# A double buffer of its own for the blocks of w_down in the up projection

## The chip, the cores and the metric

The kernel runs on one core of one Trainium2 chip. The metric is the time of one execution in microseconds of device time; three executions of the kernel before are at hand.

## The reference

One layer of a hybrid encoder block over 1024 tokens of width 1024: a convolution and attention mixer, a cross-attention into 256 memory tokens, and a gated MLP with 2816 hidden channels. Only the MLP is touched:

```python
def conv_gated_ffn(h, w_up, ffn_dw, ffn_dw_b, w_down):
    u = jnp.einsum("bsd,df->bsf", h, w_up)
    u = dwconv_centred(u, ffn_dw, ffn_dw_b)
    gate, val = u[..., :D_FF], u[..., D_FF:]
    return jnp.einsum("bsf,fd->bsd", jax.nn.gelu(gate, approximate=True) * val, w_down)
```

## The kernel before

Both projections of the MLP are done as two-by-two block products by Strassen's scheme: seven products of half-sized blocks in place of eight, paid for with sums and differences of blocks. Every float32 operand is split in a high and a low part and a block product takes three matmuls, on lines 97, 98 and 100.

The **up projection** runs in 22 rounds, one for each 128 gate and 128 value channels (`fi`). A round has seven products (against b11, b21, t2, t1, b22, t3 and t4, which are the token side's blocks and their sums). Each product has 4 steps of 3 matmuls, so a round has 84 matmuls. In the order of the program a round does this:

- `up_first(fi)` loads the gate weights `wg`, splits them (ScalarE copies the high part on line 758, GpSimd makes the low part on line 759) and runs the products b11 and b21.
- `up_operands(fi)` loads the value weights `wv`, forms sums of weight blocks on GpSimd (lines 791 to 794) and splits them (ScalarE on line 758, VectorE on line 759; the block `a22` on GpSimd).
- `down_load(fi)` loads 512 KB of `w_down` into a staging tile `wd` (line 748).
- `up_finish(fi - 1)` runs the five other products of the round before, adds them up on VectorE (line 819), applies the depthwise convolution of width 3 (lines 808 to 811), gelu and the product of gate and value (line 842), and stores the result in `act_d` (line 843).
- `down_sums(fi)` turns the four blocks of `w_down` into the four sums that the down projection will need: four subtractions of 128x256 elements in place on VectorE (line 754). It then stores them in `T_d` in DRAM (line 755). The down projection, after the 22 rounds, loads `T_d` again (line 892).

Four kinds of buffers matter. `raw` is a pool of three tiles of 512 KB, shared in the up projection by `wg`, `wv` and `wd`. `A` is a pool of 15 tiles of 1 MB: in the up projection 14 of them hold the split token operands (`b11h`, `b11l` and so on), and `acts`, the operand tiles of the down projection, and then `gF` come from the same pool, in the order of the program. `W` has seven tiles for split weights and for `u`. PSUM has four banks for the products (`psB`).

The order of the work is not that of the program alone. The program is planned ahead of time (`schedule_with_timeline_sim=True`): at each point of the planner's own estimate of time, an engine or the DMA queue of SyncE is given, of the instructions that are ready by that estimate, the one that stands earliest in the program. The order that comes out of it is fixed for each engine. On the chip each engine works its list off in order and waits at an instruction whose inputs or buffer are late. All DMAs here are issued from the one queue of SyncE (SP), in its order.

Of the kernel before, what the change touches and what calls it, by code (L numbers as in the profile page):

```python
# [8 lines left out]
F32 = mybir.dt.float32  # L9
# [8 lines left out]
NF = 22  # L18
# [15 lines left out]
def encoder_block(ctx: ExitStack, tc: tile.TileContext, x, xT, mem, w_a, w_q, w_kv, w_mkv, w_mqT,  # L34
                  w_mo, w_out, w_up, w_down, cols, rows, g10, rope, out):
    nc = tc.nc
# [10 lines left out]
    def A(shape, name, dt=F32R):  # L47
        return ap.tile([128] + shape, dt, tag="a", name=name)

    def raw(name):  # L50
        return rawp.tile([128, 1024], F32, tag="raw", name=name)
# [7 lines left out]
    def psB(name):  # L59
        return psp.tile([128, 512], F32, tag="B", name=name, bufs=4)  # L60
# [259 lines left out]
    for c in range(8):  # L320
        w = wsplit(w_mqT[c], f"wmq{c}")
        go = tmp("go")
        for g in range(2):
            p = psB("pg")
# [416 lines left out]

    T_d = drp.tile([NF // 2, 128, 4, 512], F32, name="T_d")

    wds = {}

    def down_load(fi):
        wds[fi] = raw("wd").rearrange("p (b n) -> p b n", b=4)
        nc.sync.dma_start(out=wds[fi], in_=w_down[fi // 2, :, :, fi % 2 * 256:fi % 2 * 256 + 256])

    def down_sums(fi):  # L750
        wd = wds.pop(fi)
        b11, b12, b22, b21 = [wd[:, b, :] for b in range(4)]
        for dst, in0, in1 in ((b11, b12, b11), (b12, b22, b12), (b22, b22, b11), (b21, b22, b21)):
            nc.vector.tensor_tensor(out=dst, in0=in0, in1=in1, op=ALU.subtract)  # L754
        nc.sync.dma_start(out=T_d[fi // 2, :, :, fi % 2 * 256:fi % 2 * 256 + 256], in_=wd)

    def a_split(dst, src, eng):
        nc.scalar.copy(out=dst[:, 0, :], in_=src)  # L758
# [12 lines left out]
    def up_first(fi):  # L771

        rg = rgs.pop(fi) if fi in rgs else load_raw(w_up[fi, 0], "wg")
        a1 = W([2, 2, 512], "a1")
        a_split(a1[:, 0], rg[:, H0], nc.gpsimd)
        a_split(a1[:, 1], rg[:, H1], nc.gpsimd)
        u = wp.tile([128, 2, 1024], F32, tag="w", name="u")
        q = tmp("q")
        p1, p2 = psB("p1"), psB("p2")
        product(p1, a1[:, 0], "b11")  # L780
        nc.scalar.copy(out=q[:, H0], in_=p1)
        product(p2, a1[:, 1], "b21")
        nc.vector.tensor_tensor(out=u[:, 0, H0], in0=p2, in1=q[:, H0], op=ALU.add)
        firsts[fi] = (rg, u, q)

    def up_operands(fi):

        rg, u, q = firsts.pop(fi)
        rv = load_raw(w_up[fi, 1], "wv")
        s12, s34 = tmp("s12"), tmp("s34")  # L790
        nc.gpsimd.tensor_tensor(out=s12[:, H0], in0=rv[:, H0], in1=rv[:, H1], op=ALU.add)
        nc.gpsimd.tensor_tensor(out=s12[:, H1], in0=s12[:, H0], in1=rg[:, H0], op=ALU.subtract)
        nc.gpsimd.tensor_tensor(out=s34[:, H0], in0=rg[:, H0], in1=rv[:, H0], op=ALU.subtract)
        nc.gpsimd.tensor_tensor(out=s34[:, H1], in0=rg[:, H1], in1=s12[:, H1], op=ALU.subtract)
        a2, a3 = W([2, 2, 512], "a2"), W([2, 2, 512], "a3")
        a_split(a2[:, 0], s12[:, H1], nc.vector)
        a_split(a2[:, 1], s12[:, H0], nc.vector)
        a_split(a3[:, 0], s34[:, H1], nc.vector)
        a_split(a3[:, 1], s34[:, H0], nc.vector)
        if fi % 2 == 0:  # L800
            a22[0] = W([2, 2, 512], "a22")
        a_split(a22[0][:, fi % 2], rv[:, H1], nc.gpsimd)
        ups[fi] = (a2, a3, a22[0][:, fi % 2], u, q)
# [11 lines left out]
    def up_finish(fi):  # L815
        a2, a3, a22_, u, q = ups.pop(fi)

        def add(dst, ps, other, op=ALU.add, swap=False):
            nc.vector.tensor_tensor(out=dst, in0=other if swap else ps, in1=ps if swap else other, op=op)  # L819

        p6, p5 = psB("p6"), psB("p5")
        if fi == 0:
            product(p5, a2[:, 1], "t1")
        product(p6, a2[:, 0], "t2")
        add(q[:, H0], p6, q[:, H0])
        if fi:
            product(p5, a2[:, 1], "t1")
        add(q[:, H1], p5, q[:, H0])
        p3 = psB("p3")
        product(p3, a3[:, 0], "b22")  # L830
        add(u[:, 0, H1], p3, q[:, H1])
        p7 = psB("p7")
        product(p7, a3[:, 1], "t3")
        add(q[:, H0], p7, q[:, H0])
        add(u[:, 1, H1], p5, q[:, H0])
        cg = conv3(fi, 0, u)
        nc.scalar.activation(out=u[:, 0], in_=cg, func=AF.Gelu_apprx_tanh)
        p4 = psB("p4")
        product(p4, a22_, "t4")
        add(u[:, 1, H0], p4, q[:, H0], op=ALU.subtract, swap=True)  # L840
        cv = conv3(fi, 1, u)
        nc.vector.tensor_tensor(out=u[:, 1], in0=u[:, 0], in1=cv, op=ALU.mult)
        nc.sync.dma_start(out=act_d[fi], in_=u[:, 1])
# [11 lines left out]
    for fi in range(NF + 1):  # L855
        if fi < NF:
            if fi >= UP_PRE:
                up_first(fi)
            up_operands(fi)
            down_load(fi)  # L860
        if fi:
            up_finish(fi - 1)
        if fi < NF:
            down_sums(fi)

# [205 lines left out]
```

## Time and profile before

| what | us |
|---|---|
| median of three executions | 1469.17 |
| lowest and highest of the three | 1468.13, 1473.19 |
| the profiled execution, its own time | 1470.58 |
| span of its profile (first to last instruction) | 1468.5 |
| TensorE (PE) busy in that span | 1391.3 |
| VectorE (DVE) busy | 1083.4 |
| ScalarE (ACT) busy | 699.1 |
| GpSimd (POOL) busy | 522.3 |

The engines work side by side, so the busy times don't add up to the span. 2.1 us of the profiled execution lie outside its span. The up projection takes about the stretch from 770 to 1250 us of the span.

### The profile page before, as it was taken

The numbers are of one execution on the slowest core, as the hardware profiler recorded it, in microseconds if no ns is written. First come the engines' busy times: TensorE is split into PE (matmuls) and PEld (weight loads), VectorE is DVE, ScalarE is ACT, GpSimd is POOL, SyncE is SP. The second block draws the span as 40 slices with busy tenths as digits, with TensorE's granted clock in tenths as the row PEclk, the third lists the DMA queues.
The fourth block names the chain that finished last, engine by engine and source line by source line (L and its number), as shares of the span: only waits on it lengthen the run. The fifth ranks groups of instructions, "written<-read, shape, count | busy, mean of one in ns | idle before, by whom it ended". The sixth has DMA issues, their size and how long they took to land.

```text
span 1468.5 us, 18850 instructions
## 1 busy us (share of the span) xinstructions
PE 1391.3 (95%) x7020; PEld 1168.7 (80%) x7020; DVE 1083.4 (74%) x1464; ACT 699.1 (48%) x1192; POOL 522.3 (36%) x508
## 2 busy tenths in 40 slices
PE   7999999889999999999997899999998999999996
PEld 5889988678988888888885677777787777888885
DVE  7599898899999534335468777777777678986576
ACT  6325653678888524334344433343344333544452
POOL 6628877711111414002136533444455441000003
PEclk9999999999999999999998999999999999999999
DMA  6416760000000424113222443343343348622325
GB/s 209 136 50 207 254 240 13 20 1 1 1 2 29 165 94 142 46 43 130 86 86 75 155 143 129 125 135 129 131 129 113 130 143 308 251 90 90 108 86 208
DMA packets 74059, 170.08 MB, mean 116 GB/s; under 512 B 9712, under 2 KB 32496, under 8 KB 73968
## 3 DMA queue, kind: packets, MB, share of 16 engines
q1 hardware_dynamic: 73968, 168.88, 34.2%
q8 instruction: 55, 0.90, 0.3%
q14 instruction: 36, 0.29, 0.1%
HBM read 124.82 MB, written 44.04 MB: 115 GB/s over the span
## 4 chain that ended last, share of the span: by engine, by line
PE 48%; DVE 20%; DMA 12%; issue 8%; POOL 7%; ACT 4%; SPq 1%; DVEq 0%; POOLq 0%; ACTq 0%
DMA wd<-in_w_down_dram 5%; PE yd L91 4%; PE yd L92 4%; PE yd L90 4%; PE y L98 4%; PE y L100 4%; PE y L97 4%; DVE wd L754 3%; PE pPT L81 3%; DMA T_d<-wd 2%; PE sc L100 2%; PE sc L97 2%; PE sc L98 2%; DVE u L819 2%; PE sp L524 2%
## 5 line engine op out<-in xcount | busy, mean ns | idle before, releaser
L295 DVE SCALAR_TENSOR_TENSOR cacc<-conv,col,cacc 128x1009 f32<-128x1009 f32 (+14 forms) x120 | 145.8, 1274 | 4.7 <-ACT cacc L242 4.4
L85 POOL TENSOR_SCALAR rt<-ss 128x1 f32<-128x1 f32 (+1 forms) x43 | 14.9, 347 | 367.6 <-DVE ss L899 228.3
L91 PE MATMUL yd<-op 128*128 128x512 f32 x308 | 119.9, 390 | 0.5 <-DVE op L899 0.5
L92 PE MATMUL yd<-op 128*128 128x512 f32 x308 | 119.7, 389 | 0.0
L758 ACT CAST a<-s 128x512 fp32r<-128x512 f32 x88 | 51.5, 619 | 114.4 <-PE p L100 53.8
L754 DVE TENSOR_TENSOR wd<-wd 128x256 f32<-128x256 f32 x88 | 63.8, 725 | 55.0 <-DMA wd<-in_w_down_dram 40.8
L759 POOL TENSOR_TENSOR a<-wg,a 128x512 fp32r<-128x512 f32 x44 | 61.0, 1406 | 102.5 <-ACT a L758 102.1
L90 PE MATMUL yd<-op 128*128 128x512 f32 x308 | 97.1, 389 | 0.0
L909 ACT CAST op<-acts 128x512 fp32r<-128x512 f32 x77 | 47.9, 622 | 97.7 <-PE yd L92 86.6
L899 DVE TENSOR_TENSOR op<-acts,op 128x512 fp32r<-128x512 f32 x77 | 52.9, 687 | 45.5 <-ACT op L909 45.4
L545 DVE TENSOR_TENSOR PL<-pPT,PH 128x512 fp32r<-128x512 f32 x128 | 82.7, 680 | 5.0 <-ACT PH L544 4.6
L527 DVE TENSOR_REDUCE nm<-sp 128x1 f32<-128x1024 f32 x64 | 78.0, 1219 | 3.2 <-PE sp L525 2.2
L809 DVE SCALAR_TENSOR_TENSOR c<-u,col,c 128x1023 f32<-128x1023 f32 x44 | 56.5, 1284 | 28.9 <-ACT c L808 28.9
L530 ACT ACTIVATE P<-sp,nm 128x1024 f32<-128x1024 f32 x64 | 72.2, 1129 | 8.8 <-PE pPT L81 5.1
L544 ACT CAST PH<-pPT 128x512 fp32r<-128x512 f32 x128 | 69.2, 593 | 13.5 <-PE pPT L81 12.8
L81 PE MATMUL pPT<-ident,P 128*128 128x128 f32 x512 | 69.5, 276 | 2.4 <-DVE PL L545 1.0
L759 DVE TENSOR_TENSOR a<-s,a 128x512 fp32r<-128x512 f32 x88 | 59.4, 694 | 12.3 <-ACT a L758 12.3
L91 PEld LDWEIGHTS yd<-op 128*128 128x128 f32 x308 | 57.8, 188 | 13.2 <-DVE op L899 1.3
L81 PEld LDWEIGHTS pPT<-ident,P 128*128 128x128 f32 x512 | 59.7, 142 | 10.6 <-DVE PL L545 3.1
L90 PEld LDWEIGHTS yd<-op 128*128 128x128 f32 x308 | 57.8, 188 | 12.0
L92 PEld LDWEIGHTS yd<-op 128*128 128x128 f32 x308 | 57.8, 188 | 12.0
L808 ACT ACTIVATE c<-u,col 128x1024 f32<-128x1024 f32 x44 | 53.2, 1209 | 26.9 <-DVE u L819 25.9
(341 smaller groups left out, 4401.0 us busy)
## 6 DMA issues: line engine op xcount, KB each, us to landing
wg<-in_w_up_dram SPq DMA_DIRECT2D x22, 512.0 KB, 3.7
wv<-in_w_up_dram SPq DMA_DIRECT2D x22, 512.0 KB, 4.3
wd<-in_w_down_dram SPq DMA_DIRECT2D x22, 512.0 KB, 3.9
T_d<-wd SPq DMA_DIRECT2D x22, 512.0 KB, 3.2
act_d<-u SPq DMA_DIRECT2D x22, 512.0 KB, 5.1
acts<-act_d SPq DMA_DIRECT2D x22, 512.0 KB, 8.3
st<-T_d SPq DMA_DIRECT2D x20, 512.0 KB, 3.7
wmkv_r<-in_w_mkv_dram SPq DMA_DIRECT2D x16, 512.0 KB, 4.2
```

The source lines that it names most:

```text
L81: nc.tensor.transpose(out=out_, in_=in_, identity=ident)
L90: nc.tensor.matmul(out=ps, lhsT=sh, rhs=mh, start=first, stop=False)
L91: nc.tensor.matmul(out=ps, lhsT=sh, rhs=ml, start=False, stop=False)
L92: nc.tensor.matmul(out=ps, lhsT=sl, rhs=mh, start=False, stop=last)
L97: nc.tensor.matmul(out=p, lhsT=sh, rhs=mh, start=first, stop=False)
L98: nc.tensor.matmul(out=p, lhsT=sh, rhs=ml, start=False, stop=False)
L100: ins = nc.tensor.matmul(out=p, lhsT=sl, rhs=mh, start=False, stop=last)
L295: nc.vector.scalar_tensor_tensor(out=acc[:, t0:t1_], in0=a[:, t0 + o:t1_ + o], scalar=cc(C_DW + c * 31 + j), in1=acc[:, t0:t1_], op0=ALU.m ...
L527: nc.vector.reduce_max(out=nm, in_=sp, axis=AX.X, negate=True)
L545: nc.vector.tensor_tensor(out=PL[dst], in0=p3, in1=f(PH[dst]), op=ALU.subtract)
L754: nc.vector.tensor_tensor(out=dst, in0=in0, in1=in1, op=ALU.subtract)
L759: eng.tensor_tensor(out=dst[:, 1, :], in0=src, in1=f(dst[:, 0, :]), op=ALU.subtract)
```

## The change

The blocks of `w_down` no longer come through the pool `raw`. One tile of the pool `A` becomes a double buffer `wd_b`, with one half for even and one for odd `fi`. The store to `T_d` is split off from the sums into `down_store`. The load for round `fi + 1` now stands behind the sums of round `fi` in the program, and the store of round `fi - 1` stands in round `fi`, between `up_operands(fi)` and `up_finish(fi - 1)`. The number of loads, sums and stores, and their sizes, stay as they are.

```diff
-    wds = {}
+    wd_b = A([2, 4, 256], "wd", F32)
+
+    def down_slice(dr, fi):
+        return dr[fi // 2, :, :, fi % 2 * 256:fi % 2 * 256 + 256]
 
     def down_load(fi):
-        wds[fi] = raw("wd").rearrange("p (b n) -> p b n", b=4)
-        nc.sync.dma_start(out=wds[fi], in_=w_down[fi // 2, :, :, fi % 2 * 256:fi % 2 * 256 + 256])
+        nc.sync.dma_start(out=wd_b[:, fi % 2], in_=down_slice(w_down, fi))
 
     def down_sums(fi):
-        wd = wds.pop(fi)
-        b11, b12, b22, b21 = [wd[:, b, :] for b in range(4)]
+        b11, b12, b22, b21 = [wd_b[:, fi % 2, b, :] for b in range(4)]
         for dst, in0, in1 in ((b11, b12, b11), (b12, b22, b12), (b22, b22, b11), (b21, b22, b21)):
             nc.vector.tensor_tensor(out=dst, in0=in0, in1=in1, op=ALU.subtract)
-        nc.sync.dma_start(out=T_d[fi // 2, :, :, fi % 2 * 256:fi % 2 * 256 + 256], in_=wd)
+
+    def down_store(fi):
+        nc.sync.dma_start(out=down_slice(T_d, fi), in_=wd_b[:, fi % 2])
...
             up_operands(fi)
-            down_load(fi)
-        if fi:
+        if fi == 0:
+            down_load(0)
+        else:
+            down_store(fi - 1)
             up_finish(fi - 1)
         if fi < NF:
             down_sums(fi)
+        if fi + 1 < NF:
+            down_load(fi + 1)
```

## Rows read from the trace of the kernel before

**Rows 1.** The page's head: span, then busy us, share and instructions per engine

```profile
span 1468.5 us, 18850 instructions
PE 1391.3 (95%) x7020; PEld 1168.7 (80%) x7020; DVE 1083.4 (74%) x1464; ACT 699.1 (48%) x1192; POOL 522.3 (36%) x508
```

**Rows 2.** Matmuls on t4h: duration ns min/median/max, first and last start in us

```profile
L97 PE MATMUL p<-t4h,a x88: 389/389/389, 807.3 to 1246.1; 128*128 128x512 f32 x88
```

**Rows 3.** Timeline of PE, four instructions: start us, us, line, idle before and releaser

```profile
813.03 0.50 PE L97 MATMUL p<-b11h,a 128*128 128x512 f32 x1 [2.90 <-ACT a L758]
...
1005.85 0.47 PE L97 MATMUL p<-b21h,a 128*128 128x512 f32 x1 [3.00 <-DVE q L819]
...
1112.65 0.39 PE L97 MATMUL p<-t2h,a 128*128 128x512 f32 x1
...
1123.53 0.39 PE L97 MATMUL p<-t4h,a 128*128 128x512 f32 x1
```

**Rows 4.** PE's waits from 780 to 1271 us: total us, times, longest

```profile
PE p L97 <- DVE q L819: 19.7, 9, 3.0
PE p L97 <- ACT a L758: 7.2, 4, 2.9
```

**Rows 5.** One stretch of 5 us: PE busy, granted clock, DMA share, GB/s

```profile
920.00:925.00 5.00, 1.99 (x6) 0.78 0.09 30
```

**Rows 6.** Timeline of DVE, two stretches

```profile
1000.50 1.29 DVE L809 SCALAR_TENSOR_TENSOR c<-u,col,c 128x1023 f32<-128x1023 f32 x1 [1.28 <-ACT c L808]
1003.57 1.54 DVE L754 TENSOR_TENSOR wd<-wd 128x256 f32<-128x256 f32 x1 [1.78 <-DMA wd<-in_w_down_dram]
1005.03 0.68 DVE L819 TENSOR_TENSOR q<-p,q 128x512 f32<-128x512 f32 x1
...
1066.70 0.95 DVE L899 TENSOR_TENSOR acts<-acts 128x512 f32<-128x512 f32 x1 [0.74 <-DMA acts<-act_d]
```

**Rows 7.** Timeline of POOL, two instructions

```profile
999.73 1.30 POOL L759 TENSOR_TENSOR a<-wv,a 128x512 fp32r<-128x512 f32 x1
...
1003.57 1.25 POOL L791 TENSOR_TENSOR s<-wv 128x512 f32<-128x512 f32 x1
```

**Rows 8.** Timeline of SP's queue: when each DMA was issued

```profile
4.47 1.52 SPq L422 DMA_DIRECT2D rope_t<-in_rope_dram  x2
...
791.13 0.66 SPq L748 DMA_DIRECT2D wd<-in_w_down_dram  x1
800.37 0.34 SPq L617 DMA_DIRECT2D wv<-in_w_up_dram  x1
...
808.41 0.34 SPq L617 DMA_DIRECT2D wg<-in_w_up_dram  x1
...
829.38 0.33 SPq L874 DMA_DIRECT2D acts<-act_d  x1
...
999.80 0.57 SPq L748 DMA_DIRECT2D wd<-in_w_down_dram  x1
...
1247.26 0.33 SPq L878 DMA_DIRECT2D gF<-in_rows_dram  x1
```

**Rows 9.** All instructions on wd: the sums' ns, DVE's wait before them, landing

```profile
L754 DVE TENSOR_TENSOR wd<-wd x88: 406/424/1539, 798.8 to 1215.8; 128x256 f32<-128x256 f32 x88
...
  DMA wd<-in_w_down_dram: 40.8, 15
...
DMA to landing us min/median/max: 3.2/3.7/7.9
```

**Rows 10.** DMA issues: count, KB each, median us from issue to landing

```profile
wd<-in_w_down_dram SPq DMA_DIRECT2D x22, 512.0 KB, 3.9
T_d<-wd SPq DMA_DIRECT2D x22, 512.0 KB, 3.2
```

**Rows 11.** 820 to 1220 us: busy of PE, PEld, DVE, ACT, POOL, clock, DMA share, GB/s

```profile
820.00:1220.00 400.00, 374.86 (x1600) 304.16 (x1599) 301.23 (x387) 152.60 (x213) 179.84 (x136) 0.98 0.40 132
```

**Rows 12.** The same stretch, the sums of line 754 alone: DVE busy first

```profile
820.00:1220.00 400.00, 57.64 (x80) 0.98 0.40 132
```

## The prediction

> **What bounds the kernel now.** I read the page first: PE is busy 95% of the span [rows 1], so a change can only gain where PE stands still or runs slowly. The change touches the up projection alone, so next I measured that stage by PE's own pace. In full flow, four products lie between the two last rows of the PE timeline: 48 matmuls in 1123.53 - 1112.65 = 10.88 us, 0.2267 us each [rows 3]. A round of 84 matmuls would take 19.04 us at that pace. The t4 products of the first and last round start at 807.3 and end their fourth step's first matmul at 1246.1 [rows 2]: between them lie 21 rounds and three steps, 1773 matmuls, which should take 401.9 us and take 438.8. **36.9 us are lost in the stage**, and a round takes 20.80 us. That is all that a perfect cure of the stage could give.
>
> Then I asked what ends PE's waits. The largest entry is "q L819", VectorE's add that frees a PSUM bank: 19.7 us in 9 waits, the longest 3.0; then weights that ScalarE had not split yet, 7.2 us in 4 [rows 4]. The rest of the 36.9 are smaller waits and slow running: in the 5 us around one such stop the granted clock averages 0.78 [rows 5].
>
> One stop shows the mechanism. PE waits 3.00 us before 1005.85 for the add q [rows 3]. On VectorE that add stands behind the first subtraction on `wd`, which waited 1.78 us for its load and then took 1.54 us [rows 6]. The load was issued at 999.80, while GpSimd was at the low part of a value weight block (`a<-wv`, from 999.73), whose reading frees a `raw` tile [rows 7, 8]. So `wd` gets its buffer late, lands late, and VectorE, which works in order, holds up an add that was ready. Over the stage VectorE waits 40.8 us in 15 places for `wd` [rows 9].
>
> **The change, part by part.**
>
> *Bytes and instructions.* 22 loads, 88 subtractions, 22 stores before and after: 0 us of work added or removed.
>
> *`raw` has one user less.* Two tiles a round instead of three use the three buffers. The start shows what that is worth: the second `wv` was issued only at 800.37, the third `wg` at 808.41, because the first `wd` had taken a buffer at 791.13 [rows 8], and PE then waited 2.90 us for the split of that `wg` [rows 3]. With the buffer free, `wv` moves to about 791 and `wg` to about 800, 8 to 9 us earlier, more than that wait. This is part of the 36.9, not in addition.
>
> *`wd_b` takes the 15th `A` tile.* The first half of the first `acts` was loaded into it at 829.38 [rows 8]. Now that load comes after the last store to `T_d`; it is needed at the down projection, beyond 1246, so 0 us while the last store is done well before. The first `wd` load must wait for the tile, until the token operands are split and the 15th tile is free: the first sums now start at 798.8 [rows 9], and a load issued there lands 3.9 us later [rows 10]. Between 0 and 3.9 us, once; I take 0, because it is weighed again in the next term.
>
> *The loads asked for a round ahead, the stores a round behind.* What the program says about rounds binds little, since the planner issues whatever is ready. Two rows show it: the position tables of the attention stage were loaded at 4.47, as their small buffer was free, and the first `acts` half at 829.38, some twenty rounds ahead of its place [rows 8]; VectorE even did a sum on `acts` at 1066.70, in the middle of the up projection, and waited 0.74 us for it [rows 6]. What held `wd` to its round was the shared pool, whose tiles go out in program order (`gF`, which waits for no result, was loaded only at 1247.26, behind the `acts` [rows 8]). With a buffer of its own nothing holds it. **So I expect the blocks to run ahead:** load, four sums, store, next load into the same half, as fast as it goes, in VectorE's gaps. From the rows: load 3.9 [rows 10], four sums at 57.64 / 80 = 0.72 us each, 2.9 [rows 12], store 3.2 [rows 10], together 10.0 us for a half, two halves in turn, a block per 5.0 us, 22 blocks in 110 us. VectorE's other work is (301.23 - 57.64) / 400 = 61% [rows 11, 12], 12.7 us in a round of 20.80, or 67% at PE's full pace. A planner that counts the undisturbed 0.42 us [rows 9] has 88 x 0.42 = 37 us of sums to place in the remaining 33%, which takes 112 us: the same answer from the other side. The sums will be through by about 800 + 112 = 912, in six rounds, and 15 or 16 rounds then run without any `wd` work.
>
> *What the run-ahead costs.* In those six rounds VectorE has no spare time left by plan, and the sums really take 0.72, not 0.42: 88 x 0.30 = 26 us more. The excess is seen at 1003.57: the subtraction took 1.54 us and ended only when the GpSimd instruction that began with it had ended [rows 6, 7]. Lower bound 0 (if the sums stay spread over the stage, they need 2.9 us of 6.3 spare in a round); upper bound of this term 26 (VectorE full, all of it handed on to PE). Before, 40.8 us of waits [rows 9] and 26 of excess, 67 us of VectorE's delay, cost PE at most its 36.9, 0.55 of it, as VectorE had slack; without slack I take three quarters: **20 us**.
>
> The Trainium skill ("SBUF — State Buffer", § Who interferes with whom) says the same against the change: a VectorE instruction with two SBUF inputs and a GpSimd instruction that reads SBUF exclude each other, the later one blocked until the first ends. The trace agrees (1.54 against 0.42 us). By that rule with GpSimd busy 179.84 of 400 us, bunching the sums removes no collision; it only moves them to where nothing absorbs them.
>
> *The waits on `wd`.* After the sixth round they are gone, and with them most of PE's stops. In the run-ahead, a block's load is issued by its own half's store, not by GpSimd; I count its lateness as 0 here and keep it as a rival.
>
> **Sum.** 36.9 lost before, 20 lost after: 17 us gained. Profiled execution 1470.6 - 17 = 1453.6; the median of the three is 1.4 lower, which gives **1452 us**. With the term at its bounds, 0 and 26, the same sum gives 1432 and 1458.
>
> **Rivals.**
>
> 1. *Nearly all idle goes.* The excess is absorbed and the last waits go too: loss after below 10 us, 1432 to 1442. For it: VectorE's waits for `wd` stand directly ahead of PE's stops [rows 3, 6]. Against it: six rounds without slack. The Trainium skill ("Perfetto Trace Analysis", § Optimization Strategy) reads a gap that returns on the engine that should be saturated as too few buffers; by that reading the gap goes with the added buffer, and this is the case. The trace bears it out as far as the chain above goes.
> 2. *The gap moves and nothing is won.* Run-ahead costs what the waits did: VectorE's full excess of 26 us, plus 0.5 us of lateness on each of 22 loads, makes 37: 1469, within a few us.
> 3. *Slower: the ring of load, sums, store is the bound.* In the run-ahead SP's queue holds a load until the store of the same half has landed, 3.2 us [rows 10], with `wg`, `wv` and `act_d` queued behind it, and VectorE's fixed order holds PE to the ring's pace. Landings of `wd` go up to 7.9 us when several transfers are in flight [rows 9]. At 14.5 us for a half instead of 10.0, 22 blocks cost 22 x 2.25 = 50 us against 36.9 before: 13 us slower, 1482. It decides from 13.4 us for a half on, where 22 x 1.7 = 37. Against it: DMA is busy only 40% now [rows 11].
> 4. *The double buffer doesn't work as one*, every load waiting for all work on the other half. Then a block takes 10.0 us alone, the sums are spread over 220 us, 2.9 us in each 10, and about half the excess is absorbed: 13 us lost, 24 gained, 1445.
>
> **How the numbers follow.** Forecast (8 to 25 us gained, 1444 to 1461): 0.40. Rival 1: 0.17. Rival 4: 0.05. Rival 2: 0.16. Rival 3: 0.22. About 0.3%, 4.4 us, is what can be told from no change; so faster 0.62, same 0.16, slower 0.22. The range reaches from the lower cases to two thirds of rival 3: 1434 to 1479.
>
> **What would show it right or wrong.** Right: 22 `wd` loads issued by about 930, DMA share in 800 to 930 well above 0.40, VectorE near full there, sums still at about 0.7 us, and rounds of 19 to 19.3 us after. Wrong: sums spread to 1200 (run-ahead false); rounds after 930 still near 20.8 (the waits had another cause behind them, such as `u` held until `act_d` lands); or PE's loss before 930 near 50 (rival 3).

## The result, and the profile after

| what | before | after |
|---|---|---|
| median of the executions compared (11 each), us | 1470.52 | 1463.1 |
| span of the profile, us | 1468.5 | 1460.3 |
| PE busy, us | 1391.3 | 1388.2 |
| first and last start on t4h, us | 807.3, 1246.1 | 804.2, 1238.4 |

The ratio is 0.9945 (95% interval 0.993 to 0.9959): faster by 7.4 us where 17 were forecast. One of the eleven executions before took 4892.28 us and is left out of the ratio. The predicted 1452 us is 11 us too low; the time lies inside the range.

The page of the kernel after: its head, then three DMA groups (count, KB of one, median us from issue to landing).

```profile
span 1460.3 us, 18824 instructions
PE 1388.2 (95%) x7020; PEld 1170.1 (80%) x7020; DVE 1091.1 (75%) x1464; ACT 700.4 (48%) x1192; POOL 526.4 (36%) x508
...
wd<-in_w_down_dram SPq DMA_DIRECT2D x22, 512.0 KB, 4.8
T_d<-wd SPq DMA_DIRECT2D x22, 512.0 KB, 3.3
act_d<-u SPq DMA_DIRECT2D x22, 512.0 KB, 2.9
```

The groups of instructions on t4h and on `wd` (lines are shifted by 2 to 3: the sums are now line 755, ScalarE's split 761, the adds 822, the product of gate and value 845, the store of `act_d` 846), and what VectorE waited for ahead of the sums:

```profile
L97 PE MATMUL p<-t4h,a x88: 389/389/392, 804.2 to 1238.4; 128*128 128x512 f32 x88
...
L755 DVE TENSOR_TENSOR wd<-wd x88: 408/419/1524, 800.4 to 962.0; 128x256 f32<-128x256 f32 x88
L750 SPq DMA_DIRECT2D wd<-in_w_down_dram x22: 539/551/682, 796.3 to 953.8; - x22
L758 SPq DMA_DIRECT2D T_d<-wd x22: 562/565/585, 810.4 to 962.4; - x22
...
  DMA wd<-in_w_down_dram: 14.1, 10
```

The run-ahead is there: the sums end at 962, where they lasted to 1215.8 before [rows 9], and VectorE's wait for blocks fell from 40.8 us to 14.1. Two stretches show what it does to PE (columns: stretch, its length, busy PE, PEld, DVE, ACT, POOL, granted clock, DMA share, GB/s):

```profile
820.00:980.00 160.00, 141.04 (x577) 113.26 (x576) 137.65 (x191) 54.65 (x78) 65.79 (x49) 0.93 0.60 198
980.00:1220.00 240.00, 239.47 (x1056) 197.97 (x1056) 175.44 (x205) 98.81 (x137) 114.81 (x86) 1.00 0.29 94
```

After the blocks are done, PE stands still for 0.5 us in 240, at full clock. While they run, it stands still for 19 us in 160. Its waits over the stage, 780 to 1271 us:

```profile
PE p L97 <- ACT a L761: 15.6, 5, 5.4
PE p L97 <- DVE u L822: 5.4, 1, 5.4
PE p L97 <- DVE q L822: 4.3, 3, 3.6
```

Before, most was due to VectorE's add q, 19.7 us in 9 waits [rows 4]; now it is 4.3, and ScalarE's splits have taken its place, 15.6 instead of 7.2. The largest stop, in the order of time, on the timelines of four engines of the kernel after. DVE:

```profile
909.38 1.86 DVE L755 TENSOR_TENSOR wd<-wd 128x256 f32<-128x256 f32 x2
911.71 3.07 DVE L755 TENSOR_TENSOR wd<-wd 128x256 f32<-128x256 f32 x4 [0.47 <-DMA wd<-in_w_down_dram]
914.70 1.28 DVE L812 SCALAR_TENSOR_TENSOR c<-u,col,c 128x1023 f32<-128x1023 f32 x1
...
918.95 1.21 DVE L845 TENSOR_TENSOR u<-u,c 128x1024 f32<-128x1024 f32 x1
```

SP's queue:

```profile
918.05 0.54 SPq L750 DMA_DIRECT2D wd<-in_w_down_dram  x1
918.70 0.56 SPq L758 DMA_DIRECT2D T_d<-wd  x1
919.37 0.56 SPq L617 DMA_DIRECT2D wv<-in_w_up_dram  x1
920.19 1.33 SPq L846 DMA_DIRECT2D act_d<-u  x1
```

ACT and PE, and two 5 us stretches around the end of PE's stop (PE, PEld, DVE, ACT, POOL, clock, DMA share, GB/s):

```profile
909.89 1.20 ACT L811 ACTIVATE c<-u,col 128x1024 f32<-128x1024 f32 x1
...
927.04 1.14 ACT L761 CAST a<-wv 128x512 fp32r<-128x512 f32 x2 [9.54 <-DMA act_d<-u]
928.09 1.20 ACT L811 ACTIVATE c<-u,col 128x1024 f32<-128x1024 f32 x1
929.23 1.12 ACT L761 CAST a<-wg 128x512 fp32r<-128x512 f32 x2
```

```profile
929.89 0.79 PE L97 MATMUL p<-b11h,a 128*128 128x512 f32 x1 [5.45 <-ACT a L761]
```

```profile
925.00:930.00 5.00, 0.11 (x1) 0.12 (x1) 2.23 (x4) 2.96 (x5) 2.26 (x2) 0.87 0.77 270
930.00:935.00 5.00, 4.84 (x11) 3.37 (x12) 5.00 (x7) 0.36 (x1) 4.32 (x4) 0.50 0.67 212
```

ScalarE has its second `c` ready from 911, but VectorE first does six sums, 909.38 to 914.7, and two more behind them (915.89 and 918.02). So the convolution, the product of gate and value (ends 920.16) and the store of `act_d` come 4.3 us late: 3.6 us from 911.09 to 914.70 and 0.7 for the two. The six took 4.9 us, where undisturbed ones take 0.42 each, 2.5 together; GpSimd was at work beside them from 909.54 to 913.82. That store is issued 1.5 us behind the store of a block and right behind the load of `wv`, and lands around 927. Only then is `u`'s tile of the pool `W` free for the split `wv`; behind that split, in ScalarE's fixed order, stands the split of `wg` that PE needs. PE stops for 5.45 us, and then runs 11 matmuls in the next 5 us at half clock (1.2 GHz), where full flow has 22.

### The profile page after: what moved, and what is told of

Same layout as the page of the kernel before. It is cut to its first block, busy times and chain, and to the rows that moved or that the text cites. A ratio compares the mean times of both kernels' runs of the same rounds, so it can differ in the third digit from the quotient of the medians.

```text
span 1460.3 us, 18824 instructions
## 1 busy us (share of the span) xinstructions
PE 1388.2 (95%) x7020; PEld 1170.1 (80%) x7020; DVE 1091.1 (75%) x1464; ACT 700.4 (48%) x1192; POOL 526.4 (36%) x508
## 4 chain that ended last, share of the span: by engine, by line
PE 67%; DVE 15%; DMA 8%; ACT 3%; POOL 3%; issue 3%; SPq 0%; POOLq 0%; DVEq 0%; ACTq 0%
PE p L97 5%; PE p L98 5%; PE p L100 5%; PE yd L90 5%; PE yd L91 5%; PE yd L92 5%; PE y L100 3%; PE y L98 3%; PE y L97 3%; DVE wd L755 3%; PE pPT L81 3%; DMA wd<-in_w_down_dram 3%; DMA T_d<-wd 2%; PE sc L100 2%; PE sc L97 2%
## 5 line engine op out<-in xcount | busy, mean ns | idle before, releaser
L812 DVE SCALAR_TENSOR_TENSOR c<-u,col,c 128x1023 f32<-128x1023 f32 x44 | 56.6, 1285 | 41.0 <-ACT c L811 40.8
L762 DVE TENSOR_TENSOR a<-s,a 128x512 fp32r<-128x512 f32 x88 | 69.3, 801 | 18.0 <-ACT a L761 18.0
L527 DVE TENSOR_REDUCE nm<-sp 128x1 f32<-128x1024 f32 x64 | 78.1, 1220 | 2.7 <-PE sp L525 1.8
L544 ACT CAST PH<-pPT 128x512 fp32r<-128x512 f32 x128 | 69.4, 594 | 13.1 <-PE pPT L81 12.3
L755 DVE TENSOR_TENSOR wd<-wd 128x256 f32<-128x256 f32 x88 | 61.6, 714 | 14.4 <-DMA wd<-in_w_down_dram 14.1
```

What stands on the lines that cost most here:

```text
L527: nc.vector.reduce_max(out=nm, in_=sp, axis=AX.X, negate=True)
L762: eng.tensor_tensor(out=dst[:, 1, :], in0=src, in1=f(dst[:, 0, :]), op=ALU.subtract)
```

## The experiments

Times are medians of 4 executions (p1 7, o1 10, the changed kernel 11); the ratio is to the kernel before, run beside it on the same chip (1470.5 to 1472.7 us).

| kernel | us | ratio, 95% |
|---|---|---|
| after | 1463.1 | 0.993 to 0.9959 |
| n1, no blocks | 1427.78 | 0.9696 to 0.9722 |
| d1, sums without transfers | 1450.2 | 0.9844 to 0.9873 |
| t1, transfers without sums | 1442.89 | 0.9789 to 0.9818 |
| p1, one load a round | 1465.31 | 0.9959 to 0.9982 |
| s1, sums behind the product | 1429.36 | 0.9691 to 0.9742 |
| p2, sums and loads held | 1428.1 | 0.9687 to 0.9732 |
| g1, sums on GpSimd | 1452.75 | 0.9857 to 0.9904 |
| o1, own buffer, order of before | 1463.31 | 0.9934 to 0.997 |
| x1, sums held to an earlier point | 1445.65 | 0.9807 to 0.9853 |
| b1, kernel before with sums held | 1436.86 | 0.9749 to 0.9799 |
| w1, two blocks a round, held | 1436.56 | 0.9735 to 0.9793 |
| w2, the same from round 1 on | 1430.83 | 0.9697 to 0.9741 |

**n1: the floor.** From the changed kernel (here and in d1 the down projection also reads `w_down` in place of `T_d`; that line, and in n1 the one of the buffer, are not shown):

```diff
-        if fi == 0:
-            down_load(0)
-        else:
-            down_store(fi - 1)
+        if fi:
             up_finish(fi - 1)
-        if fi < NF:
-            down_sums(fi)
-        if fi + 1 < NF:
-            down_load(fi + 1)
```

> Leaves out the loads, sums and stores of w_down's blocks; the down projection reads w_down in place of T_d, so its result is another. Theory R (the changed kernel still loses 32 us in the up projection because the 22 blocks now run bunched in its first 175 us): without them PE loses under 10 us in the stage, 1432 to 1442 us. Rival F (the first eight rounds lose their time anyway, through the start of the stage and the seven W tiles): the stops before 975 us stay, 1455 to 1463 us.

1427.78 us, 35.3 below the changed kernel, lower than any of the theories gave. The t4h products start between 805.5 and 1202.9, in 397.4 us:

```profile
L97 PE MATMUL p<-t4h,a x88: 389/389/389, 805.5 to 1202.9; 128*128 128x512 f32 x88
```

From 780 us on, PE's only stop of over 1.5 us is one of 4.1 us, for the low part of the token operand t2, as the stage begins. So the handling of the blocks is all that PE loses in this stage.

**d1 and t1: the two halves of the cost.** d1 drops the stores and all loads but two:

```diff
             down_load(0)
+            down_load(1)
         else:
-            down_store(fi - 1)
             up_finish(fi - 1)
         if fi < NF:
             down_sums(fi)
-        if fi + 1 < NF:
-            down_load(fi + 1)
```

> Keeps all 88 subtractions but loads only the first two blocks and stores none (the down projection reads w_down in place of T_d, so its result is another). If the bunched sums on VectorE, with their collisions with GpSimd, are the cost: 1450 to 1462 us, with PE's stops still ahead of 975 us. If the traffic and the waits for it are the cost: like the kernel without the blocks, 1432 to 1442 us.

t1 drops the sums alone:

```diff
-        if fi < NF:
-            down_sums(fi)
```

> Keeps all 22 loads and 22 stores but leaves out the subtractions, so T_d holds w_down's blocks as they are. If traffic is the cost (act_d lands late, the tile of u comes free late, ScalarE's splits wait): 1448 to 1460 us, with the stops bunched in the first 80 to 100 us of the stage. If VectorE's sums are the cost: 1432 to 1442 us.

d1 takes 22.4 us more than n1, t1 15.1 more; together 37.5, and the changed kernel has 35.3. d1 stands at the lower end of the expectation for the sums, t1 between its two. Neither alone is the cause. How the changed kernel's 35.3 divide is not shown by this, since each half alone runs ahead faster than both together: the sums of d1 and the stores of t1 are through by 915 and 906, in the changed kernel by 962. The sums of d1, and the stores of t1:

```profile
L755 DVE TENSOR_TENSOR wd<-wd x88: 404/411/1549, 802.6 to 915.2; 128x256 f32<-128x256 f32 x88
...
L758 SPq DMA_DIRECT2D T_d<-wd x22: 553/562/573, 803.5 to 905.9; - x22
```

In t1, with VectorE free of sums, PE's largest stop has the same last links. SP's queue and ACT of t1:

```profile
864.62 2.76 SPq L758 DMA_DIRECT2D T_d<-wd  x2
868.24 0.59 SPq L750 DMA_DIRECT2D wd<-in_w_down_dram  x1
868.87 0.65 SPq L846 DMA_DIRECT2D act_d<-u  x1
```

```profile
874.17 0.62 ACT L761 CAST a<-wv 128x512 fp32r<-128x512 f32 x1 [8.10 <-DMA act_d<-u]
```

The product of gate and value ended at 863.71, but the store of `act_d` was issued at 868.87, behind stores and a load of blocks in the queue's fixed order, and landed 5.1 us later.

**p1: pace the loads.** The load of block fi+1 may be issued only behind the store of `act_d` of round fi-1 (`issue_after` fixes the place in the planned order):

```diff
             down_load(0)
+            down_load(1)
         else:
             down_store(fi - 1)
-            up_finish(fi - 1)
+            stored = up_finish(fi - 1)
...
-        if fi + 1 < NF:
-            down_load(fi + 1)
+        if fi and fi + 1 < NF:
+            with tc.issue_after(stored.ins):
+                down_load(fi + 1)
```

> The load of block fi + 1 is held, on SP's queue, behind the store of act_d of round fi - 1, so that the blocks can no longer run ahead; all work is done. Theory R: PE's stops go as they did after 975 us in the changed kernel, 1434 to 1446 us. Rival F: nothing changes, 1458 to 1466 us. Rival L (sums placed right behind a load that lands later than planned hold up VectorE, bunched or not): stops of 1 to 3 us come back in most rounds, 1455 to 1470 us.

1465.31 us: the run-ahead is gone (sums from 803.6 to 1235.7, VectorE waits 0.2 us for blocks), and the time is 2.2 us above the changed kernel's. Spreading the blocks does not help by itself, and late loads are not the cost here. In a typical round the sums now stood at GpSimd's low part of `wg` and ahead of an add into `u` (two of them took 2.94 us from 1015.68 on), so that ScalarE's `c` came late and the split of `wg` behind it. That gave the next theory: what counts is which instruction stands behind the sums.

**s1 and p2: put the sums behind the product.** The sums of round fi are held until the product of gate and value of round fi-1 (line 845) has been issued; loads and stores stay as in the change.

```diff
             down_load(0)
+            down_sums(0)
         else:
             down_store(fi - 1)
-            up_finish(fi - 1)
-        if fi < NF:
-            down_sums(fi)
+            mul = up_finish(fi - 1)
+        if fi and fi < NF:
+            with tc.issue_after(mul.ins):
+                down_sums(fi)
```

> The changed kernel, with the four VectorE sums of round fi held (from round 1 on) until the product of gate and value of round fi-1 has been issued; loads and stores of the blocks stay where the change put them, so that the sums pace them to one block a round. The product is where GpSimd has nothing to do for about 7 us (in the run with one load a round GpSimd was idle from 1007 to 1013.9). Theory P (what costs is where the sums fall, beside GpSimd's halves of the splits, and two blocks a round in flight when the values to be split come back): the sums pay 0.4 us each instead of up to 1.5, VectorE's wait for them falls, the splits start on time: 1432 to 1442 us. Rival C (the cost of the sums and of the traffic is paid wherever they are put, 35 us over the kernel without blocks): 1458 to 1466 us, as with one load a round.

p2 adds p1's hold on the loads (and, not shown, the load of block 1 in the first round):

```diff
-        if fi + 1 < NF:
-            down_load(fi + 1)
+        if fi and fi + 1 < NF:
+            with tc.issue_after(stored.ins):
+                down_load(fi + 1)
```

> The kernel of the run before (sums of round fi behind the product of round fi-1), and the load of block fi+1 held until the store of the activations of round fi-1 has been issued. Theory P: the sums' place decides and the load was paced already: within 3 us of the run with the sums held alone. Rival Q (loads that are free to go ahead of the activations' store delay it on its queue): 5 to 12 us faster than the run with the sums held alone. Theory C as before: 1458 to 1466 us.

1429.36 and 1428.1 us: 34 and 35 us below the changed kernel, with all of its work, and within 2 us of the kernel without blocks. s1 is 3 us below the lowest time of its theory P. One round of s1 on DVE, GpSimd and SP's queue:

```profile
913.59 1.22 DVE L845 TENSOR_TENSOR u<-u,c 128x1024 f32<-128x1024 f32 x1
914.73 0.42 DVE L755 TENSOR_TENSOR wd<-wd 128x256 f32<-128x256 f32 x1
915.71 0.69 DVE L786 TENSOR_TENSOR u<-p,q 128x512 f32<-128x512 f32 x1 [0.57 <-PE p L100]
916.32 0.42 DVE L755 TENSOR_TENSOR wd<-wd 128x256 f32<-128x256 f32 x1
...
912.99 1.30 POOL L797 TENSOR_TENSOR s<-wg,s 128x512 f32<-128x512 f32 x1
920.20 2.99 POOL L762 TENSOR_TENSOR a<-wg,a 128x512 fp32r<-128x512 f32 x2 [5.91 <-ACT a L761]
...
914.84 0.33 SPq L846 DMA_DIRECT2D act_d<-u  x1
```

The store of `act_d` is issued at 914.84, as soon as the product is done. GpSimd ended its last sum of weights at 914.3 and has nothing until 920.2, so that a sum takes its undisturbed 0.42 us; the 88 sums take 39.1 us instead of 61.6. Rival Q of p2 falls: holding the loads as well changes nothing that can be told.

**g1: the sums on GpSimd.** From the changed kernel:

```diff
-            nc.vector.tensor_tensor(out=dst, in0=in0, in1=in1, op=ALU.subtract)
+            nc.gpsimd.tensor_tensor(out=dst, in0=in0, in1=in1, op=ALU.subtract)
```

> The changed kernel with the four sums of each half on GpSimd instead of VectorE, everything else as the change left it. If the 22 us of the sums are VectorE's time (and the locks between it and GpSimd show only there), VectorE's chain gets them back and what is left is the traffic: 1440 to 1448 us. If GpSimd's halves of the splits then come late instead, since a sum there takes some 1 us and four of them 4 us ahead of a split: PE waits for the low half of the values by GpSimd (1.1 us in 2 waits so far) grow to over 15 us, and the time is 1455 to 1475 us.

1452.75 us, between the two expectations: 10.4 us better than the changed kernel, still 25 over n1. The run-ahead stays (sums to 971.1, median 0.74 us each there, not the 1 us expected), and from 785 us on PE's waits are again for ScalarE's splits, 12.1 us in 5. GpSimd's own lateness is 2.8 us in 2 waits. Freeing VectorE helps less than placing the sums.

**o1: the buffer without the new order.** Load in its round, store right behind the sums:

```diff
-        if fi == 0:
-            down_load(0)
-        else:
-            down_store(fi - 1)
+        if fi < NF:
+            down_load(fi)
+        if fi:
             up_finish(fi - 1)
         if fi < NF:
             down_sums(fi)
-        if fi + 1 < NF:
-            down_load(fi + 1)
+            down_store(fi)
```

> The double buffer of the change alone: load of block fi in round fi, its sums and at once its store, in the program order of the kernel before. If the order of loads and stores of the change binds nothing, since blocks run ahead of the rounds as soon as the buffer is free of the staging tile: 1460 to 1466 us, blocks done by about 960. If the load a round ahead and the store a round behind matter: away from the changed kernel by over 4 us, with VectorE's wait for the loaded block well over the changed kernel's 14 us.

1463.31 us, and sums from 800.3 to 961.4: by time and by the sums' place the same kernel. A round ahead or behind in the program binds nothing; the buffer is the whole change.

**x1: paced, but in the wrong place.** s1 with the hold on an earlier instruction of the same round:

```diff
-        add(u[:, 0, H1], p3, q[:, H1])
+        first = add(u[:, 0, H1], p3, q[:, H1])
...
-            with tc.issue_after(mul.ins):
+            with tc.issue_after(first.ins):
                 down_sums(fi)
```

> The kernel with the sums held, but held to an earlier point of the same round: behind the first sum of gate products into u (product of a3's first half with b22) instead of the product of gate and value. The sums are still paced to one block a round; on VectorE three of the four now stand ahead of the first convolution step, where it waits 1.28 us for ScalarE and where GpSimd has its four operations on the second half (split of wg 2.55 us, s 1.3 us each). Theory P1 (the place counts: the sums have to be where GpSimd is idle): each takes 0.7 to 1.5 us instead of 0.42, three take 2 to 4.5 us in a gap of 1.28, the first convolution comes 1 to 3 us late in each round, and PE has 0.5 to 2 us a round less cover: 1440 to 1465 us. Rival P2 (one block a round is what counts, the place does not): 1427 to 1434 us.

1445.65 us, 16 above s1. The sums stand ahead of the convolution and beside GpSimd; DVE and GpSimd of x1:

```profile
1005.55 3.68 DVE L755 TENSOR_TENSOR wd<-wd 128x256 f32<-128x256 f32 x3
1009.15 1.28 DVE L812 SCALAR_TENSOR_TENSOR c<-u,col,c 128x1023 f32<-128x1023 f32 x1
...
1004.72 2.80 POOL L762 TENSOR_TENSOR a<-wg,a 128x512 fp32r<-128x512 f32 x2 [7.01 <-ACT a L761]
1007.47 1.47 POOL L794 TENSOR_TENSOR s<-wv 128x512 f32<-128x512 f32 x1
```

Three sums take 3.68 us where s1 has a gap of 1.28 (the mean of the 88 is 884 ns, in s1 444). P1 holds, P2 falls.

**b1: the place without the buffer.** The kernel before, with the hold of s1 and nothing else (the load stays in the staging tile, the store directly behind the sums):

```diff
-            up_finish(fi - 1)
-        if fi < NF:
-            down_sums(fi)
+            mul = up_finish(fi - 1)
+        if fi == 0:
+            down_sums(0)
+        elif fi < NF:
+            with tc.issue_after(mul.ins):
+                down_sums(fi)
```

> The kernel before, with its staging tile, its load in the round and its store behind the sums, and one thing changed: the sums of round fi are held until the product of gate and value of round fi-1 has been issued. Theory P (the sums' place is what the rounds were missing, the buffer is not): PE's stops of 36.9 us fall to under 8 and the time is 1430 to 1440 us, near the 1429.4 of the kernel with both. Rival S (the staging tile shared with gate and value halves is a stop of its own, since a block held longer keeps their loads back): PE waits for splits that wait for the halves, 1445 to 1475 us.

1436.86 us. Together with the others this is a square: the buffer gives 7.4 us where the sums are free (1470.5 to 1463.1) and 7.5 where they are held (1436.9 to 1429.4); the place gives 34 either way (33.7 and 33.7 from the same four medians). The kernel before itself moved by up to 2.2 us beside these runs; the ratios of the table, which take that out, give 8 for the buffer and 33 for the place, each to within some 5 us. The time is that of theory P, but the buffer is not nothing: a part of what is left to it shows in PE of b1, a stop of the kernel before [rows 3] that the shared `raw` makes and that is 1.10 us in s1:

```profile
814.71 0.50 PE L97 MATMUL p<-b11h,a 128*128 128x512 f32 x1 [2.77 <-ACT a L758]
```

**w1 and w2: a run-ahead in the right place.** Two blocks a round, all eight sums behind the product; w1 does blocks 0 and 1 in the first round without a hold, w2 only block 0. The core of w2:

```diff
+            mul = up_finish(fi - 1)
+            two = [k for k in (2 * fi - 1, 2 * fi) if k < NF]
+            with tc.issue_after(mul.ins):
+                for k in two:
+                    down_sums(k)
+            for k in two:
+                down_store(k)
+                if k + 2 < NF:
+                    down_load(k + 2)
```

> Two blocks a round in the first eleven rounds: their eight sums behind the product of gate and value of the round before, their stores and the next two loads behind them. This is the pace of the changed kernel's run ahead with the place of the best kernel so far. If the pace is what costs (the 15 us of the traffic without sums: 18 to 25 GB/s more in each us while the activations' store and the halves of the splits want to land): 1440 to 1450 us, with PE stops that begin at the ScalarE splits and with the activations' store landing late in the first eleven rounds. If the place is all that counts: 1428 to 1434 us.

> Two blocks a round behind the product, as in the run before, but only block 0 in the first round, so that no eight sums stand among the splits of round 1 (there PE stopped 5.01 us at 814.98 for a sum into u, and the stage took 405.8 us against 398.3). Theory: with the place right the doubled pace costs nothing, and the 7.2 us were that one stop and the clock after it: 1428 to 1433 us, no stop of PE over 3 us after 805. Rival (the pace itself costs the 7 us): 1434 to 1440 us, as before.

w1 came out between its expectations, at 1436.56; after one stop of 5.01 us at 814.98, where eight sums stood among the splits of round 1, PE was busy 159.65 of the 160 us from 820. w2 removes that stop: 1430.83 us. Its loads, and its windows:

```profile
L750 SPq DMA_DIRECT2D wd<-in_w_down_dram x22: 563/592/672, 798.7 to 1003.1; - x22
...
820.00:980.00 160.00, 160.00 (x707) 132.40 (x706) 136.88 (x206) 64.85 (x92) 81.95 (x58) 1.00 0.59 191
```

Against the same stretch of the changed kernel: VectorE as busy (136.88 and 137.65), DMA as busy (0.59 and 0.60), PE 160.00 instead of 141.04, with 707 matmuls instead of 577. So that much load on VectorE and that much traffic do not by themselves cost PE anything. The pace of the blocks is not quite that of the change, though: one in 9.7 us ((1003.1 - 798.7) / 21), against 7.5 there; VectorE and the DMA are as busy since the rounds go by faster. Three blocks a round in the right place were not run. (The 18 to 25 GB/s of the expectation are in no row: from 820 to 980 us n1 moves 88 GB/s and w2 191.)

## Why the prediction was wrong

**The bound, 36.9 us lost before: too small by 5.4.** The products b11 and b21 of the next round stand ahead of a round's t4, and the last round has no next one, so that 24 of the 1773 matmuls are not between the two rows. 1749 x 0.2267 is 396.5, and n1's 397.4 confirms it. The loss was 42.3 us, and is 37.7 after the change (434.2 - 396.5); by the prediction's own count 36.9 and 32.3. Of the 37.7, 29 fall from 820 to 980 us, where 577 matmuls ran and full pace has 706: 19 us of standing still and 10 of running slowly, at a mean granted clock of 0.93.

**`raw` has one user less: right.** (One row was misread, without harm: two low parts of value weights run on GpSimd from 998.41, and the load of 999.80 left when the first had ended, not during the one from 999.73 [rows 7].) The second `wv` and the third `wg` were issued by 788.9 and at 799.31 instead of 800.37 and 808.41 [rows 8]. PE's first stop is no longer ScalarE's (it is 5.42 us for an add into u, behind sums of blocks 0 and 1). b1 against s1 puts the buffer's worth at 7.5 us, the whole gain of the change.

**The 15th tile at 0: right.** The first `acts` is loaded at 965.74 behind the last store to `T_d`, long before the down projection.

**Blocks run ahead: right, but slower.** Done at 962, not 912: a block per 7.5 us ((953.8 - 796.3) / 21) instead of 5.0. From 980 on the rounds run at PE's full pace, as forecast. Two more of the signs came: from 800 to 930 the DMA share was 0.64, and a sum took 0.70 us in the mean (61.6 / 88).

**What the run-ahead costs, 20 us: this step failed.** The loss after is 32.3 us by the same count, 12.3 more than the term; less the 3.1 us by which the stage starts earlier, that is 9.2 of the 9.6 us that the gain fell short. By the right count the term should have been 37.7; with 42.3 lost before and the 20 as taken, the same sum would have given 22.3 us gained and 1447 us, so that the bound's error hid a part of this one, by luck. Two things were wrong in the term. Its size left out the lateness counted as 0 (t1: 15.1 us for the transfers alone, as the store of `act_d` is issued and lands late and holds `u`'s tile; the prediction looked for lateness at the loads of `wd`) beside the sums (d1: 22.4, near the 20 taken). And its reason was wrong: VectorE "without slack" was said to hand its excess to PE. VectorE was busy 110.17 of the 130 us from 800 to 930, 85%, and in w2, as busy, it hands on nothing. A sum costs PE time where a critical chain stands behind it on VectorE (adds into u, convolution, product, then the store of `act_d` and the split that waits for it), and next to nothing where that chain has just been handed on.

**The rivals.** Rival 2 (nothing won, 37 us of loss) was nearest in mechanism, excess and lateness together, though the lateness was that of the store of `act_d` and not of the loads; its size only looks the same, 37.7, because the loss before was 42.3. Rival 3 fell: at 7.5 us a block a half takes 15 us, past the 13.4 from which it should have been slower than before, and it was not. Rival 4 fell with the sums done by 962. Rival 1's time was reached and passed (1429 us in s1), but not by a buffer: the runs put 7.4 of 41 us down to the buffer and 34 to the order. The rule cited for it (the Trainium skill, "Perfetto Trace Analysis", § Optimization Strategy) names too few buffers as what can be behind a returning gap. The traces bear that out for the smaller part only. A sum took 444 ns in the mean where GpSimd is mostly idle (s1), 884 where it works (x1). The rule that the prediction took from the Trainium skill ("SBUF — State Buffer", § Who interferes with whom) is that a VectorE instruction with two SBUF inputs and a GpSimd instruction that reads SBUF lock each other out; these means agree with it. The prediction's "it only moves them to where nothing absorbs them" overlooked that a quiet place exists in each round.

**What stays open.** How t1's 15.1 us divide between the wait in SP's queue and the late landing. How the place's 34 us divide: behind the product of gate and value, the critical chain has just left VectorE and GpSimd is idle too, so that the 88 sums take 39.1 us instead of 61.6, and no run has the one without the other. And the planner shifts other instructions with each edit. From the first product against b11 to the last against t4, PE's matmuls stand in the same order in n1, t1 and s1, which can be compared without that doubt. In every second round these three put seven matmuls of t2 between the last of b11 and the rest of b21, 1.6 us of work while b21 waits for an add; so does b1 from its third such round on. The kernel before has none there from its third such round on, x1 none at all, p1 three in all but the first. So a part of what p1 and x1 lose, and of the 34 us between the kernel before and b1, may come from there. In the run-ahead it is not the cause: the changed kernel has 0, 0, 11 and 9 in its first four such rounds, and w2, which runs at full pace, 7, 0, 8, 9 and 9.

## What to carry to other kernels

When background work shares an in-order engine with the critical chain, look at which instruction stands behind it, and hold it until that chain has handed on its result; here that was worth 34 us, and the deeper buffer 7.4. Under this planner, which issues whatever is ready, the new buffer did not smooth the work: it let it run ahead, and its transfers took places in the queue ahead of a store that others wait for. Before calling an engine or the traffic the bound, compare a stretch with the same load and another order.

## What the runs showed of the hardware that was not expected

The time of a 512 KB store went with what was issued just ahead of it, at nearly the same mean traffic: the store of `act_d`, 820 to 980 us, minimum, median and maximum us to landing, in the changed kernel at 198 GB/s:

```profile
DMA to landing us min/median/max: 3.1/4.9/7.7
```

and in w2 at 191 GB/s:

```profile
DMA to landing us min/median/max: 2.6/3.1/4.4
```

In the changed kernel five of the seven were issued within 1.8 us behind another transfer of the queue, and these took 4.5 to 7.7 us to land; the two others took 3.1 each. In w2 none of the nine stood closer than 2.6 us behind another. Whether the issue behind another or the transfers that run at once slow them, no run separates. The issue of the store on SP alone took up to 1.47 us in the changed kernel and at most 0.33 in w2.
